# A seven-product SwiGLU in a two-layer decoder: another order for the begun pair, a shorter lead for weights, and three moved sums

## The chip, the cores and the metric

The kernel runs on one core of one Trainium2 chip. A core has a matrix engine (PE; its weight loads are shown apart as PEld), a vector engine (DVE), a scalar engine (ACT), a general engine (POOL) and a queue processor (SP) that mostly starts transfers. Each engine works through its own instructions strictly in the order in which the program lists them; engines meet only at semaphores. The metric is the device time of one execution in microseconds; the smaller, the better. Times of one kernel lie close together (955.57 to 956.49 us in three runs of the kernel before).

## The reference

Two decoder layers over 512 tokens of width 1024. Layer 0 mixes tokens by causal pooling, layer 1 by differential attention; behind each mixer stands a dense SwiGLU block, and each of the four steps ends in a LayerNorm of `ALPHA * x + step(x)`. The change touches the SwiGLU blocks, which both layers have:

```python
D_MODEL = 1024; SEQ = 512; DEPTH = 2; D_FF = 2816
def _swiglu(x, w_gate, w_up, w_down):
    return (jax.nn.silu(x @ w_gate) * (x @ w_up)) @ w_down
...
        x = _layernorm(ALPHA * x + h, ln_mix_g[i], ln_mix_b[i])
        x = _layernorm(ALPHA * x + _swiglu(x, w_gate[i], w_up[i], w_down[i]), ln_ffn_g[i], ln_ffn_b[i])
```

All of it is float32.

## The kernel before

**Float32 in two parts.** PE multiplies in a format with fewer bits, so each float32 operand is held as a high part (a copy that is rounded, made by ACT: a CAST) and a low part (the rest, made by DVE as a subtraction: a "low"). A product then takes three matmuls: high by high, high by low, low by high. So every block of 128x1024 weights costs one transfer from HBM (into a buffer named `raw`, of which there are five), one CAST on ACT, one low on DVE, and it occupies one of six pairs of weight buffers until PE has used it.

**Seven products in place of eight.** The 2816 hidden rows are 22 blocks of 128. Block k and block k + 11 make up pair k (k from 0 to 10). Pairs 0 to 2 are computed plainly (`plain`: a gate and an up product for each block). Pairs 3 to 10 (`SPLIT`) go through `strassen(k)`. There the two halves of the model width, gate against up, and the two halves of the tokens are combined in Strassen's manner: seven half products replace eight. Their weights are sums of rows of the weight array, which DVE forms ("sum" steps, L660, in place in the raw buffers). Their right operands are quarters of x, or sums of quarters, which `sums_of_x` prepares once (parts `xs`, made at L717 and L720). The seven are named P1, Q5, P6, Q3, P7, P2, Q4, and this is also their order in `GATE`. Each half product is 24 matmuls (`half_product`).

**Banks.** A half product accumulates into a bank of PSUM: P1, P6, P7 and Q4 into A, Q5 and Q3 into C, P2 into B. Between two products on one bank the running sum is read out: ACT copies A to B after P1 (L965), A to `hid` after P6 (L969) and C to `hid` after Q5 (L967); DVE takes C after Q3 (L971) and A after P7 (L973). The next product on that bank waits for that reading. Pair 3 is "begun" in the early part of the block, where tokens of the first half are ready before the others: its P1 and P2 are computed there, so the loop in `strassen(3)` has five products left: Q5, P6, Q3, P7, Q4.

**Who makes weights when.** A weight block that is ready to multiply is a "chunk"; chunks are numbered in the order in which PE takes them. In layer 0 and layer 1 alike 0 to 13 are the plain ones and the early two, 14 to 18 the five of pair 3, 19 to 25 those of pair 4, and so on, seven a pair, to 67. `steps` is a list, written by hand for a pair, of sums, CASTs and lows. `ahead(upto)` carries out steps until all chunks below `upto` are done. After product j, `strassen` calls `ahead(j + 6)`. What this emits lands in DVE's and ACT's queues ahead of whatever is emitted later, the reading of later banks included.

**Other work in the same queues.** `sum_terms(k)` (L774, L775) adds blocks of the down weights and ACT stores the results to HBM (L779). `sum_hidden(k)` makes two sums of hidden rows for the down products: four DVE operations on 128x256 (L800 to L803), a CAST on ACT (L805), a low on DVE (L807) and a store by ACT (L809). Its tiles `u` and `v` have one buffer each. It is queued after every pair in `behind`, and `catch_up` carries each queued job one step further after every product. The down products (L1023) come last in the block. ACT starts its own transfers, and its queue stands still while such a start waits.

**The end of the pooling mixer.** `ready(n)` prepares the first n weight rows while the mixer ends. `norm(0, 3)` (L217) normalizes the last quarter of the tokens, after POOL has raised the variance to a power (L208).

## Time and profile before

| | us |
|---|---|
| median of three runs | 956.07 |
| the profiled execution | 954.77 |
| its span (first to last instruction) | 953.0 |
| PE busy in the span | 925.6 (97%) |
| DVE busy | 801.3 (84%) |
| ACT busy | 521.2 (55%) |
| POOL busy | 126.1 (13%) |

The profiled execution is 1.3 us under the median and 1.8 us over its own span. PE is busy nearly throughout, so a time can change by PE's idle time and by the clock at which PE runs (the granted clock, whose mean is 0.988 of full). Layer 0's SwiGLU lies between 35 and 372 us of the span, layer 1's from about 606 us to the end; attention lies between them. A view of waits tells for which engine's instruction another engine stood idle; a timeline gives start, length and the idle time just before; the chain is the work that set the end, in order of time.

### The profile page before, as it was taken

How to read it: one execution, taken by the hardware profiler on the slowest of the kernel's cores; microseconds unless marked ns; L12 is line 12 of the kernel's file. 1: busy time of each engine (PE TensorE's matmuls, PEld its weight loads, DVE VectorE, ACT ScalarE, POOL GpSimd, SP SyncE). 2: the span in 40 equal slices, each digit the busy share in tenths (PEclk: the TensorE clock that was granted, in tenths of full speed). 3: DMA queues.
4: the chain of work that ended last, by engine and by line, in shares of the span. 5: the costliest groups of instructions: out<-in, count | busy, mean ns of one | idle time of the engine just before them, and what ended most of it. 6: DMA issues, size and time to landing. Idle time of an engine off the chain costs nothing.

```text
span 953.0 us, 15072 instructions
## 1 busy us (share of the span) xinstructions
PE 925.6 (97%) x5758; PEld 831.5 (87%) x5758; DVE 801.3 (84%) x1172; ACT 521.2 (55%) x826; POOL 126.1 (13%) x152
## 2 busy tenths in 40 slices
PE   9999969999999999999999999999889999999996
PEld 8898869999998888888888888988789999988885
DVE  8978988999978687968989777879979999878678
ACT  6652444555455456776878854832435455564450
POOL 4111111110000201100111100211111110001101
PEclk9999989999999999999999999999989999999998
DMA  8497898886868988876676521595888985778952
GB/s 235 165 283 244 232 304 250 261 243 189 281 196 258 358 283 249 224 190 169 145 153 161 168 71 67 171 319 168 270 246 262 266 261 205 252 254 271 362 173 88
DMA packets 86614, 213.21 MB, mean 224 GB/s; under 512 B 15204, under 2 KB 26724, under 8 KB 86542
## 3 DMA queue, kind: packets, MB, share of 16 engines
q1 hardware_dynamic: 43996, 119.26, 38.3%
q0 software_dynamic: 18768, 58.20, 25.3%
q10 hardware_dynamic: 23778, 34.78, 9.9%
q8 instruction: 45, 0.74, 0.3%
q14 instruction: 27, 0.22, 0.1%
HBM read 175.50 MB, written 36.72 MB: 223 GB/s over the span
## 4 chain that ended last, share of the span: by engine, by line
PE 82%; DVE 12%; issue 3%; ACT 2%; DMA 0%; POOL 0%; DVEq 0%; ACTq 0%; POOLq 0%
PE A L867 19%; PE P L1023 13%; PE C L867 8%; PE Q L1023 6%; PE B L867 5%; PE va L1173 2%; PE s L1242 2%; PE q L158 2%; PE q L160 2%; PE k L158 2%; PE k L160 2%; PE q L159 2%; PE k L159 2%; DVE raw L660 2%; PE vc L1173 1%
## 5 line engine op out<-in xcount | busy, mean ns | idle before, releaser
L660 DVE TENSOR_TENSOR raw<-raw,raw 128x1024 f32<-128x1024 f32 x64 | 78.1, 1221 | 1.0
L132 ACT CAST xs<-hid 128x512 fp32r<-128x512 f32 (+1 forms) x60 | 34.7, 581 | 24.3 <-DVE hid L837 24.3
L133 DVE TENSOR_TENSOR xs<-hid,xs 128x512 fp32r<-128x512 f32 (+1 forms) x60 | 38.4, 642 | 7.8 <-ACT xs L132 7.8
L1262 ACT ACTIVATE p<-p,mn 128x128 f32<-128x128 f32 (+3 forms) x64 | 35.2, 552 | 14.1 <-DVE mn L1257 14.1
L258 ACT ACTIVATE y<-pt,bT,gT 128x128 f32<-128x128 f32 x72 | 27.0, 455 | 27.9 <-PE pt L244 27.8
L768 POOL DMA_DIRECT2D b<-in_wall x20 | 14.0, 706 | 183.7 <-DMA tsum<-b 122.5
L829 POOL DMA_DIRECT2D xs<-ssum x24 | 17.4, 725 | 142.3 <-PE Q L1023 68.8
L208 POOL TENSOR_TENSOR rs<-rs,mhalf 128x1 f32<-128x1 f32 x16 | 12.1, 760 | 141.5 <-DVE rs L207 102.0
L768 POOL DMA_DIRECT2D hid<-in_wall x24 | 18.7, 824 | 88.1 <-DMA tsum<-hid 45.4
L1257 DVE CUSTOM_DVE_ANT_0 p<-s,bias 128x128 f32<-128x128 f32 (+3 forms) x64 | 28.0, 485 | 1.1 <-PE s L1242 1.1
L971 DVE TENSOR_TENSOR hid<-C,hid 128x512 f32<-128x512 f32 x16 | 11.0, 690 | 17.7 <-PE C L867 15.1
L133 DVE TENSOR_TENSOR xt<-y,xt 128x512 fp32r<-128x512 f32 x18 | 12.2, 689 | 13.7 <-ACT xt L132 13.7
L867 PE MATMUL A<-xt,g_18h 128*128 128x256 f32 x32 | 9.3, 392 | 14.7 <-DVE hid L973 14.7
L978 ACT ACTIVATE sg<-A 128x512 f32<-128x512 f32 x16 | 9.6, 597 | 24.9 <-PE A L867 24.9
L199 DVE BATCH_NORM_STATS2 st<-res 128x6 f32<-128x512 f32 x32 | 22.2, 694 | 1.1
L805 ACT CAST v<-u 128x512 fp32r<-128x512 f32 x22 | 13.7, 621 | 14.7 <-DVE u L803 14.7
L717 ACT CAST xs<-hid 128x1024 fp32r<-128x1024 f32 x8 | 8.4, 1051 | 23.7 <-DVE hid L729 17.3
L867 PEld LDWEIGHTS A<-xt,g_18h 128*128 128x128 f32 x32 | 7.7, 294 | 15.1 <-DVE hid L973 15.1
L967 ACT COPY hid<-C 128x512 f32<-128x512 f32 x16 | 9.4, 586 | 20.5 <-PE C L867 20.5
L769 POOL DMA_DIRECT2D hid<-in_wall x12 | 14.8, 1233 | 41.8 <-DMA hid<-in_wall 41.8
L701 DVE TENSOR_TENSOR hid<-sg,u 128x512 f32<-128x512 f32 x12 | 8.2, 684 | 12.5 <-PE u L160 7.3
L1276 DVE SCALAR_TENSOR_TENSOR p<-p,sm,p 128x128 f32<-128x128 f32 (+3 forms) x32 | 17.6, 551 | 1.1
(1218 smaller groups left out, 3653.3 us busy)
## 6 DMA issues: line engine op xcount, KB each, us to landing
raw<-in_wall SPq DMA_DIRECT2D x126, 512.0 KB, 4.9
r<-tsum SPq DMA_DIRECT2D x40, 512.0 KB, 4.5
hid<-in_wall POOLq DMA_DIRECT2D x36, 512.0 KB, 5.9
b<-in_wall POOLq DMA_DIRECT2D x30, 512.0 KB, 6.0
r<-in_wall SPq DMA_DIRECT2D x30, 512.0 KB, 5.5
tsum<-hid ACTq DMA_DIRECT2D x24, 512.0 KB, 6.6
ssum<-v ACTq DMA_DIRECT2D x22, 512.0 KB, 3.7
tsum<-b ACTq DMA_DIRECT2D x20, 512.0 KB, 5.4
```

The costliest lines, as they stand in the source:

```text
L132: nc.scalar.copy(dst_h, src)
L133: (low or nc.vector).tensor_tensor(dst_l, src, dst_h.bitcast(F32), op=ALU.subtract)
L158: nc.tensor.matmul(acc, ah, bh, start=start, stop=False)
L159: nc.tensor.matmul(acc, ah, bl, start=False, stop=False)
L160: nc.tensor.matmul(acc, al, bh, start=False, stop=stop)
L660: tt(t, raws[pair[0]], raws[pair[1]], op=ALU.add)
L768: nc.gpsimd.dma_start(out=t[:, j], in_=src[:, j])
L867: nc.tensor.matmul(o, w[:, c], x[:, kk, :], start=start and f + kk + e == 0, stop=stop and (f, kk, e) == (1, 3, 2), skip_group_check=True,)
L1023: nc.tensor.matmul(accs[s], x[:, k, r], y[:, c], start=first and k == 0 and e == 0, stop=last and k == m - 1 and e == 2, skip_group_check= ...
L1173: nc.tensor.matmul(accs[s], a[:, kk, t], b[:, c], start=p in ("P1", "Q5", "P2") and kk + e == 0, stop=p in ("Q4", "Q3", "P2") and (kk, e) ...
L1257: nc.vector.tensor_tensor_reduce(out=p, in0=accs[c], in1=biases[h][:, w - 1 :: -1] if w < S else biases[h][:, ::-1], op0=ALU.add, op1=ALU. ...
L1262: nc.scalar.activation(p, p, AF.Exp, bias=mn[:, q, c : c + 1], scale=-1.0, accum_out=sm[:, q, c : c + 1],)
```

## The change

It has six parts; all but the fourth and fifth act in both layers.

1. The five products left of pair 3 now come in the order of `BEGUN`: P6, Q5, P7, Q3, Q4. With the banks as they are, A, C, A, C, A: before it was C, A, C, A, A. The silu of the finished gate part moves to the head of `strassen(3)`. The steps of this pair are listed in a new order that fits.
2. The lead of the weights shrinks: `ahead(j + 4)` after all products of pair 3 and after P1, Q5 and P6 of the others; `j + 5` after Q3, P7, P2 and Q4 up to pair 9; `j + 6` there in pair 10.
3. `sum_hidden(2)` and `sum_hidden(3)` are no longer queued behind their own pairs, but behind Q3 of pair 6 and of pair 8 (`SPARED`).
4. In layer 0 `ready(7)` before `norm(0, 3)` prepares the weights of pair 3's P1 there, as `w6`, and no longer as chunk 4 behind it.
5. P1 of the begun pair takes its 24 matmuls in another order (`high_first`): all 16 with the high weights, then the 8 with the low ones. (In layer 1 too.)
6. In `sums_of_x` the low of P6's operand comes one step earlier and that of P7's one later.

```diff
@@ -49,6 +49,8 @@
 SPLIT = (3, 4, 5, 6, 7, 8, 9, 10)
 EARLY = (2, 1)
 GATE = ("P1", "Q5", "P6", "Q3", "P7", "P2", "Q4")
+SPARED = {2: 6, 3: 8}
+BEGUN = ("P6", "Q5", "P7", "Q3", "Q4")
 PAIRS = [(0, 2), (2, 2), (4, 2), (6, 2), (8, 2), (10, 1)]
 
 
@@ -520,6 +522,7 @@
         ready(6)
         summed(3, 0, 1)
         spread_of(0, 3)
+        ready(7)
         norm(0, 3)
 
         nc.scalar.copy(far, lines_bank[:HEADS, NEAR - 1 :])
@@ -625,18 +628,22 @@
                 c = [row(4 * k + i) for i in range(4)]
                 todo = [(c[0], ()), (c[0], (c[0], c[1])), (c[0], (c[0], c[2])), (c[2], ())]
                 todo += [(c[1], (c[1], c[2])), (c[3], ()), (c[0], (c[0], c[3]))]
-                for m, chunk in enumerate(todo):
-                    if (k, m, "pair") not in number:
-                        number[k, m, "pair"] = len(chunks)
-                        chunks.append(chunk)
-                if k > SPLIT[0]:
+                begun = k == SPLIT[0]
+                for p in BEGUN if begun else GATE:
+                    m = GATE.index(p)
+                    number[k, m, "pair"] = len(chunks)
+                    chunks.append(todo[m])
+                if not begun:
                     step("cast", number[k, 0, "pair"])
-                for w in (
+                order_of = (
+                    "sum 1, cast 1, sum 4, cast 3, cast 4, low 1, sum 2, cast 2, low 2, low 4, "
+                    "low 3, sum 6, cast 6, low 6"
+                    if begun else
                     "low 0, sum 1, cast 1, sum 4, cast 3, cast 4, low 1, sum 2, cast 2, low 3, "
                     "low 2, sum 6, cast 5, cast 6, low 4, low 5, low 6"
-                ).split(", "):
-                    if k > SPLIT[0] or w[-1] not in "05":
-                        steps.append((w[:-2], number[k, int(w[-1]), "pair"]))
+                )
+                for w in order_of.split(", "):
+                    steps.append((w[:-2], number[k, int(w[-1]), "pair"]))
             uses = {}
             for kind, j in steps:
                 c, pair = chunks[j]
@@ -737,9 +744,9 @@
                 yield
                 tt(r3, r3, r2, op=ALU.add)
                 high(3, r3)
+                low(1, r2)
+                yield
                 low(2, r0)
-                yield
-                low(1, r2)
                 yield
                 low(3, r3)
                 yield
@@ -856,20 +863,23 @@
             def both(t):
                 return t.rearrange("p (f t) -> p f t", f=2)
 
-            def half_product(acc, j, left, start, stop):
+            def half_product(acc, j, left, start, stop, high_first=False):
                 h, l = halves[j]
                 xh, xl = left
-                for f in range(2):
-                    o = acc[:, f * 256 : (f + 1) * 256]
-                    for kk in range(4):
-                        c = slice((4 * f + kk) * P, (4 * f + kk + 1) * P)
-                        for e, (w, x) in enumerate(((h, xh), (h, xl), (l, xh))):
-                            nc.tensor.matmul(
-                                o, w[:, c], x[:, kk, :],
-                                start=start and f + kk + e == 0,
-                                stop=stop and (f, kk, e) == (1, 3, 2),
-                                skip_group_check=True,
-                            )
+                terms_of = ((h, xh), (h, xl), (l, xh))
+                places = [(f, kk) for f in range(2) for kk in range(4)]
+                if high_first:
+                    todo = [(f, kk, w, x) for w, x in terms_of for f, kk in places]
+                else:
+                    todo = [(f, kk, w, x) for f, kk in places for w, x in terms_of]
+                for i, (f, kk, w, x) in enumerate(todo):
+                    c = slice((4 * f + kk) * P, (4 * f + kk + 1) * P)
+                    nc.tensor.matmul(
+                        acc[:, f * 256 : (f + 1) * 256], w[:, c], x[:, kk, :],
+                        start=start and i == 0,
+                        stop=stop and i == len(todo) - 1,
+                        skip_group_check=True,
+                    )
 
             lefts = {
                 "P1": [quarter(0, i, 0) for i in range(2)],
@@ -909,7 +919,7 @@
                             behind.append(sum_hidden(0))
                 if not lo:
                     bankA, bankB = bank(f"A{layer}_{SPLIT[0]}"), bank(f"B{layer}")
-                    half_product(bankA, number[SPLIT[0], 0, "pair"], lefts["P1"], True, False)
+                    half_product(bankA, number[SPLIT[0], 0, "pair"], lefts["P1"], True, False, True)
                     if "P1" in late:
                         late["P1"]()
                     nc.scalar.copy(both(g3), both(bankA))
@@ -935,7 +945,7 @@
                     weight_sums()
                 if f == 3:
                     load_terms(3)
-                if f % 2:
+                if f % 2 and k not in SPARED:
                     behind.append(sum_hidden(k))
 
             def strassen(k):
@@ -949,14 +959,12 @@
                 def tile_of(i):
                     return keep.tile([P, S], F32, tag="y", name=f"sg{layer}_{k}_{i}", bufs=2)
 
-                for m, p in enumerate(GATE):
-                    if begun and p in ("P1", "P2"):
-                        if p == "P2":
-                            g0 = g3
-                            nc.scalar.activation(g0, g0, AF.Silu)
-                        continue
+                if begun:
+                    g0 = g3
+                    nc.scalar.activation(g0, g0, AF.Silu)
+                for p in BEGUN if begun else GATE:
                     acc = banks[names[p]]
-                    j = number[k, m, "pair"]
+                    j = number[k, GATE.index(p), "pair"]
                     half_product(
                         acc, j, lefts[p], p in ("P1", "Q5"), p in ("Q4", "Q3", "P2")
                     )
@@ -976,8 +984,10 @@
                     else:
                         g1 = tile_of(1)
                         nc.scalar.activation(both(g1), acc, AF.Silu)
-                    ahead(j + 6)
+                    ahead(j + (4 if begun or p in ("P1", "Q5", "P6") else 5 if k < SPLIT[-1] else 6))
                     catch_up()
+                    if p == "Q3" and k in SPARED.values():
+                        behind.extend(sum_hidden(i) for i in SPARED if SPARED[i] == k)
                     if p == "P2":
                         nc.scalar.activation(both(g0), acc, AF.Silu)
                     elif p == "Q4":
@@ -985,7 +995,8 @@
                         tt(second, both(g1), second, op=ALU.mult)
                 if k < HALF - 1:
                     weight_sums()
-                behind.append(sum_hidden(k))
+                if k not in SPARED:
+                    behind.append(sum_hidden(k))
 
             f = early
             while f < FB:
```

Three places show what this does to the queues. The first is DVE's queue around the reading of bank A after P7 of pair 3, in layer 0 (in layer 1 the rows are alike). `g0_19l` is a low of chunk 19; a row that writes `raw` and reads two `raw` is a sum. Before:

```order
L801 TENSOR_TENSOR hid0_531<-hid0_531 128x256
L802 TENSOR_TENSOR u0_2_1252<-hid0_531 128x256
L803 TENSOR_TENSOR u0_2_1252<-u0_2_1252,hid0_531 128x256
L660 TENSOR_TENSOR raw20_1078<-raw20_1078,raw21_1135 128x1024
L660 TENSOR_TENSOR raw21_1135<-raw21_1135,raw22_1198 128x1024
L666 TENSOR_TENSOR g0_20l_1285<-raw20_1078,g0_20h_1284 128x1024
L971 TENSOR_TENSOR hid0_531<-C0_3_1211,hid0_531 128x2x256
L660 TENSOR_TENSOR raw20_1078<-raw20_1078,raw22_1198 128x1024
L666 TENSOR_TENSOR g0_22l_1289<-raw22_1198,g0_22h_1288 128x1024
L666 TENSOR_TENSOR g0_21l_1323<-raw20_1078,g0_21h_1322 128x1024
L807 TENSOR_TENSOR v0_2_1253<-u0_2_1252,v0_2_1253 128x2x256
L973 TENSOR_TENSOR hid0_531<-hid0_531,A0_3_678 128x2x256
```

And after the change, where L981 is the line that was L973, and L979 the line that was L971:

```order
L667 TENSOR_TENSOR raw16_924<-raw16_924,raw19_1033 128x1024
L673 TENSOR_TENSOR g0_18l_1269<-raw16_924,g0_18h_1268 128x1024
L981 TENSOR_TENSOR hid0_537<-hid0_537,A0_3_678 128x2x256
L673 TENSOR_TENSOR g0_19l_1272<-raw20_1078,g0_19h_1271 128x1024
L979 TENSOR_TENSOR hid0_537<-C0_3_1205,hid0_537 128x2x256
L667 TENSOR_TENSOR raw20_1078<-raw20_1078,raw21_1195 128x1024
L667 TENSOR_TENSOR raw21_1195<-raw21_1195,raw22_1263 128x1024
L673 TENSOR_TENSOR g0_20l_1330<-raw20_1078,g0_20h_1329 128x1024
L667 TENSOR_TENSOR raw20_1078<-raw20_1078,raw22_1263 128x1024
L673 TENSOR_TENSOR g0_22l_1334<-raw22_1263,g0_22h_1333 128x1024
L673 TENSOR_TENSOR g0_21l_1368<-raw20_1078,g0_21h_1367 128x1024
L994 TENSOR_TENSOR hid0_537<-g3_0_551,hid0_537 128x2x256
```

The reading of A moved up past the lows of chunks 19 to 22, three sums, the reading of C and all of `sum_hidden(2)`.

The second place is ACT's queue from the end of pair 6 into pair 7, in layer 0. Before:

```order
L982 ACTIVATE sg0_6_0_2067<-B0_679 128x512
L978 ACTIVATE sg0_6_1_2093<-A0_6_1870 128x512
L663 CAST g0_45h_2096<-raw35_1936 128x1024
L663 CAST g0_46h_2099<-raw32_1731 128x1024
L965 COPY B0_679<-A0_7_2107 128x512
L779 DMA tsum0_533<-b0_7_1664 128x2x512 x2
L967 COPY hid0_531<-C0_7_2108 128x2x256
L663 CAST g0_47h_2176<-raw36_1968 128x1024
L805 CAST v0_6_2144<-u0_6_2143 128x2x256
L969 COPY hid0_531<-A0_7_2107 128x2x256
```

And after:

```order
L812 CAST v0_2_2018<-u0_2_2017 128x2x256
L992 ACTIVATE sg0_6_0_2047<-B0_679 128x512
L986 ACTIVATE sg0_6_1_2082<-A0_6_1844 128x512
L973 COPY B0_679<-A0_7_2089 128x512
L816 DMA ssum0_540<-v0_2_2018 512x1x256
L786 DMA tsum0_539<-b0_7_1635 128x2x512 x2
L975 COPY hid0_537<-C0_7_2090 128x2x256
L670 CAST g0_45h_2155<-raw35_1970 128x1024
L670 CAST g0_46h_2158<-raw32_1739 128x1024
L812 CAST v0_6_2124<-u0_6_2123 128x2x256
L977 COPY hid0_537<-A0_7_2089 128x2x256
```

The CASTs of chunks 45 and 46 went from before the three readings of banks to between the second and the third, and the CAST and the store of the spared `sum_hidden(2)` came in; chunk 47's CAST follows behind.

The third place is DVE's queue at the end of the pooling mixer. Before:

```order
L205 BN_AGGR mv0_3_515<-st0_3_511 128x2
L207 TENSOR_SCALAR rs0_3_517<-mv0_3_515 128x1
L217 TENSOR_SCALAR res_67<-res_67,mv0_3_515,rs0_3_517 128x1024
L666 TENSOR_TENSOR g0_4l_573<-raw6_330,g0_4h_572 128x1024
L666 TENSOR_TENSOR g0_5l_576<-raw7_482,g0_5h_575 128x1024
```

And after:

```order
L207 BN_AGGR mv0_3_515<-st0_3_511 128x2
L209 TENSOR_SCALAR rs0_3_517<-mv0_3_515 128x1
L135 TENSOR_TENSOR w6l_523<-raw6_330,w6h_522 128x1024
L219 TENSOR_SCALAR res_67<-res_67,mv0_3_515,rs0_3_517 128x1024
L673 TENSOR_TENSOR g0_5l_579<-raw7_482,g0_5h_578 128x1024
```

The low of P1's weights changed places with the normalization of the last quarter.

## The prediction

> **What bounds the kernel now.** I read the page first, then the waits of PE, then stretches of the clock and the chain of waits, and last the timelines of DVE and ACT.

> ```profile
> span 953.0 us, 15072 instructions
> PE 925.6 (97%) x5758; PEld 831.5 (87%) x5758; DVE 801.3 (84%) x1172; ACT 521.2 (55%) x826; POOL 126.1 (13%) x152
> PE 82%; DVE 12%; issue 3%; ACT 2%; DMA 0%; POOL 0%; DVEq 0%; ACTq 0%; POOLq 0%
> ```

> PE is busy for all but 27.4 us of its span, so the change, which takes no matmul away, can win idle time and clock only. Two waits hold most of the idle time (columns: total, times, longest):

> ```profile
> PE A L867 <- DVE hid L973: 14.7, 2, 7.3
> PE A L867 <- DVE g_4l L666: 2.3, 1, 2.3
> PEld o L158 <- DVE mn L1257: 2.5, 7, 0.4
> ```

> The first is Q4 of the begun pair, once in each layer, waiting until DVE has read bank A after P7. The second is P1 of that pair in layer 0, waiting for its low weights. Such idle time also costs clock. Stretches (length, PE, PEld, DVE, ACT, POOL, then the granted clock), and pieces of the chain:

> ```profile
> 46.45:49.86 3.41, 3.29 (x15) 3.29 (x16) 2.40 (x4) 0.00 (x0) 0.41 (x1) 0.50 0.95 292
> 124.95:131.78 6.83, 3.23 (x15) 3.23 (x16) 6.38 (x7) 1.68 (x2) 1.47 (x2) 0.50 0.63 182
> 691.57:698.39 6.82, 4.46 (x21) 4.46 (x22) 5.17 (x6) 0.63 (x1) 1.16 (x3) 0.50 0.85 246
> 372.00:606.00 234.00, 233.73 (x1246) 194.12 (x1245) 188.99 (x404) 169.71 (x351) 30.26 (x35) 1.00 0.59 148
> ```

> ```profile
> 46.57 4.34 PE A L867 x22
> 51.78 2.87 PE B L867 x24
> 54.65 2.88 PE g L683 x24
> 128.55 7.43 PE A L867 x48
> 150.38 5.76 PE A L867 x48
> 693.93 7.97 PE A L867 x48
> ```

> After each of the three gaps the clock stands at 0.50 for a while. 24 matmuls take 2.88 us at full clock. So the 22 after the first gap lost 4.34 - 22/24 x 2.87 = 1.7, and the 48 after the two others 7.43 - 5.76 = 1.7 and 7.97 - 5.76 = 2.2.

> **What the begun order removes.** The five products start with this row and follow without a gap, so three of them end at 109.55 + 3 x 2.88 = 118.2 and four at 121.1.

> ```profile
> 109.55 0.40 PE L867 MATMUL C<-xs,g_14h 128*128 128x256 f32 x2
> 115.69 1.22 DVE L666 TENSOR_TENSOR g_18l<-raw,g_18h 128x1024 fp32r<-128x1024 f32 x1
> 117.96 0.42 DVE L800 TENSOR_TENSOR u<-hid 128x256 f32<-128x256 f32 x1
> 119.55 2.48 DVE L660 TENSOR_TENSOR raw<-raw,raw 128x1024 f32<-128x1024 f32 x2
> 121.95 1.22 DVE L666 TENSOR_TENSOR g_20l<-raw,g_20h 128x1024 fp32r<-128x1024 f32 x1
> 127.21 0.68 DVE L807 TENSOR_TENSOR v<-u,v 128x512 fp32r<-128x512 f32 x1
> 127.81 0.68 DVE L973 TENSOR_TENSOR hid<-hid,A 128x512 f32<-128x512 f32 x1
> 95.00 1.05 ACT L663 CAST g_14h<-raw 128x1024 fp32r<-128x1024 f32 x1 [5.62 <-DVE raw L660]
> ```

> Before, P7 is the fourth (121.1), DVE reads it at 127.81, and Q4 can go at 128.5: 7.4 late. DVE is not waiting there; its queue is full. After, P7 is the third, and DVE has only to be through with the low of chunk 18. What stands ahead of that low is, by the order, the same set of operations as before, which ended at 115.69, but three of them now wait for ACT. The low of chunk 14 follows its own sum and so waits for a CAST of 1.05 (1.2 us with the hand-overs, some 0.2 more for its weight buffer); the low of chunk 18 likewise (1.1); the third wait was there before. The low thus starts at 115.69 + 2.5 = 118.2, and DVE reads A at 118.2 + 1.2 = 119.4, done at 120.1. Q4 is due at 121.1. So the whole stall goes, with 1.0 us to spare, in both layers: 14.7 us, and with it the slow clock, 1.7 + 2.2.

> From there on the walk goes through pair 4, since DVE is late: low 19, C, two sums, low 20, sum, lows 22 and 21 lead from 120.1 to about 129.0; P6 of pair 4 needs low 21 at 121.1 + 3 x 2.88 = 129.7. Next come the two gate products of `hid` and `sum_terms`, to 131.7. ACT's store of those sums waits for this and the copy of bank C stands behind it, done at 132.8; Q3 is due at 132.6. I take 0.2 us of new wait a layer.

> **What the lead costs later.** One regular pair, with T the end of Q4 of the pair before (173.4 here):

> ```profile
> 173.46 0.60 ACT L978 ACTIVATE sg<-A 128x512 f32<-128x512 f32 x1 [0.98 <-PE A L867]
> 175.55 0.68 DVE L984 TENSOR_TENSOR hid<-sg,hid 128x512 f32<-128x512 f32 x1
> 179.22 0.59 ACT L967 COPY hid<-C 128x512 f32<-128x512 f32 x1 [1.47 <-PE C L867]
> 182.09 0.59 ACT L969 COPY hid<-A 128x512 f32<-128x512 f32 x1 [0.55 <-PE A L867]
> 185.04 0.69 DVE L971 TENSOR_TENSOR hid<-C,hid 128x512 f32<-128x512 f32 x1 [1.28 <-PE C L867]
> ```

> DVE's only idle time in these 20.16 us is the 1.28. The operations are the same after the change, so a regular pair keeps it. With the new order I get: L994 at T + 2.1 as now; the sums of terms done at T + 4.7, so the copy of C done at T + 5.7 (Q3: T + 8.6); sums of hidden rows to T + 6.3, a sum to T + 7.4, the CAST of that sum and of `v` to T + 9.0, the copy of A at T + 9.6 (P7 is due at T + 11.5, 1.9 to spare). DVE reads C at T + 11.6, then two lows, and A at T + 14.5, done 2.1 before Q4. No wait.

> In pairs 7 and 9 DVE arrives 2.2 us later, since a spared sum (1.6 + 0.6, by 117.96 to 119.55 and 127.21 to 127.81) now stands before the end of pairs 6 and 8: the copy of A is done at T + 11.75, and P7 waits 0.25. That CAST of `v` also waits until the spared store, which leaves at T + 4.9, has landed, as `v` has one buffer. Landings (least, median, most) of `v`, the first row in the regular pairs, the second around the begun pair, and of rows of weights in the regular pairs:

> ```profile
> DMA to landing us min/median/max: 3.2/3.3/3.9
> ```

> ```profile
> DMA to landing us min/median/max: 3.4/5.5/7.6
> ```

> ```profile
> DMA to landing us min/median/max: 3.5/4.9/5.4
> ```

> The pairs in question are regular: landed at T + 8.2, ahead of the CAST at T + 10.5. I cost it at nothing; the cover goes if landing takes over 5.6, and at 7.6 P7 waits 2 us more, four times. DVE catches up by its 1.28 within the next pair. In pair 10 two lows of down weights and two of `hid` (about 3.5 us) now stand between the readings of C and A, which is then done at T + 17.6; Q4 is due at T + 17.3: 0.3.

> New waits: 0.2 + 0.25 + 0.25 + 0.3 = 1.0 a layer, 2.0 in all. Each is a difference of two sums of many terms, so between 0 (all covered) and about 1 apiece (8 in all). At 0.4 us, as in attention, waits leave the clock at 1.00.

> [...]

> **The low of P1 in layer 0.**

> ```profile
> 43.69 0.15 DVE L207 TENSOR_SCALAR rs<-mv 128x1 f32<-128x1 f32 x1
> 44.57 0.81 DVE L217 TENSOR_SCALAR res<-res,mv,rs 128x1024 f32<-128x1024 f32 x1 [0.73 <-POOL rs L208]
> 45.30 1.22 DVE L666 TENSOR_TENSOR g_4l<-raw,g_4h 128x1024 fp32r<-128x1024 f32 x1
> ...
> 61.98 1.22 DVE L236 TENSOR_TENSOR res<-res,gb 128x1024 f32<-128x1024 f32 x1
> ```

> ```profile
> 39.26 0.42 SPq L187 DMA_DIRECT2D gb<-in_lnb  x1
> ```

> The low now runs from 43.8 to 45.0, partly in DVE's 0.73 of waiting for POOL; the normalization slips by 0.5 to 45.1 to 45.9. P1 was due at 46.57 - 2.3 - 2 x 0.12 = 44.0 and asks for lows after 16 matmuls, at 45.9: no wait, end at 46.9, where the transposes need the normalized rows (45.9). The order of the 24 costs nothing: 24 matmuls by parts take 2.88 too (54.65). So PE gains 2.3 + 1.7 = 4.0. It stays ahead if DVE and ACT follow, and they do: their next work is the transposed tiles. Between nothing kept and all, I take all. The gamma and beta loads start one row of weights later than at 39.3, and are first needed at 62.0. The swap in `sums_of_x` moves a low by 1.14 us, and both stand before their products: nothing.

> **The sum.** 14.7 + 1.7 + 2.2 + 4.0 - 2.0 = 20.6 us. From the profiled execution, 954.77, this makes 934.2; from the median, which is 1.3 above it, 956.07 - 20.6 = 935.5.

> **The rivals.**
> 1. The front gain does not carry: DVE is nearly without gaps from there to the begun pair, and DMA engines are 0.95 busy at 46 to 50 us. Then 4.0 less: 939.5. Against it: DVE's gaps before the begun pair end with PE's results, or with a silu of them:

> ```profile
> 77.18 0.69 DVE L701 TENSOR_TENSOR hid<-sg,u 128x512 f32<-128x512 f32 x1 [0.95 <-PE u L160]
> 89.41 0.69 DVE L701 TENSOR_TENSOR hid<-sg,u 128x512 f32<-128x512 f32 x1 [1.61 <-ACT sg L700]
> ```

> 2. Short waits cost clock or the store of `v` lands late in pairs 7 and 9. Eight waits at 1.7 of clock are 13.6 (949.1); four landings at 7.6 are 8 (943.5), or with the clock 15 (950). For it: 2.3 us were enough for the clock. Against it: the clock of 1.00 in attention. [...]
> 3. The change doesn't do what it says: DVE reaches bank A too late all the same. With 1.0 to spare, a DVE 3 us later in both layers leaves two gaps of 2 with 1.7 of clock each: 7.4 less, 943. With as much delay as now, only the 4.0 is left: 952.
> 4. Slower: the third row of weights of each pair is asked for later. Its buffer comes free with a low that moves to T + 8.7 (now about T + 2), and the sum that needs it is due at T + 16.3: a lead of 7.6 us. Landing takes 3.5 to 5.4, so I see no wait. DVE's 1.28 covers the first excess; beyond 8.9 us every pair loses the rest. To eat 20.6 us over 14 pairs, 1.5 each, landings must take 10.4 throughout; at 10.6 the time is 935.5 + 14 x 1.7 = 959.

> **How the numbers follow.** No change can be told from one within 0.2% (1.9 us). My forecast has 0.62 (933 to 938), rival 1 0.12 (938 to 941), rival 2 0.11 (943 to 950), rival 3 0.08 (943 to 952), rival 4 and other slower ends 0.05 (959), no change 0.02. The low end, 932.5, is the gain without any new wait, 956.07 - 22.6 = 933.5, less 1 for the spread of the runs. The high end, 944, takes in rivals 1 and the nearer ends of 2 and 3, and leaves out under 0.2. Faster: 0.62 + 0.12 + 0.11 + 0.08 = 0.93.

> **What would show it.** Right: PE's wait for the reading of A after P7 is gone, the clock has no stretch at 0.50 between 46 us and the tail, P1's matmuls end about 4 us earlier, and DVE keeps an idle time near 1.3 before the reading of C. Wrong: PE's waits for ACT's copies of A or C sum to over 3 us, a CAST of `v` waits for a DMA, or DVE waits for a DMA at a sum of rows.

## The result, and the profile after

The kernel after takes 939.68 us (median of six runs, 938.56 to 942.77), beside 956.28 for the kernel before on the same chip (six runs, 954.72 to 956.79). The ratio is 0.9834, with a 95% interval of 0.9818 to 0.985: faster by 1.7%, or 16.6 us. The forecast was 935.5, a gain of 20.6; the measured time lies within the range, and 4.0 us of the gain are missing. The profiled execution took 938.56 us, the shortest of the six. Its span and busy times, from the page:

```profile
span 936.8 us, 15062 instructions
PE 923.9 (99%) x5758; PEld 828.1 (88%) x5758; DVE 801.2 (86%) x1172; ACT 517.6 (55%) x826; POOL 127.1 (14%) x152
```

PE's idle time has gone from 27.4 to 12.9 us. DVE and ACT do nearly as much work as before. PE's waits in the SwiGLU blocks (total, times, longest):

```profile
PE A L877 <- DVE hid L981: 0.9, 2, 0.6
PE A L877 <- ACT hid L977: 0.8, 5, 0.2
PE C L877 <- ACT hid L975: 0.6, 1, 0.6
PE g L690 <- ACT xt L134: 0.2, 1, 0.2
```

The 14.7 us at the reading of A after P7 and the 2.3 at P1 are gone; L981 still stands here, but for pair 10, where a new wait was forecast. And the clock (length, PE, PEld, DVE, ACT, POOL, granted clock, DMA share, GB/s):

```profile
7.51:932.52 925.01, 918.35 (x5736) 822.86 (x5735) 795.45 (x1165) 512.86 (x819) 124.84 (x140) 1.00 0.74 228
```

No stretch at 0.50 is left between the start and the tail. So all that was to go has gone. Where the 16.2 us between the two spans come from, and where some are lost again, is seen in the starts of PE's products (the first row of each product in the two timelines of PE; the lead is the time before minus the time after):

| start of | before | after | lead of after |
|---|---|---|---|
| the first stretch at full clock | 5.49 | 7.51 | (starts later) |
| the second group of pooling matmuls with low weights | 7.24 | 8.06 | -0.82 |
| the transposes behind P1, layer 0 | 50.74 | 47.58 | 3.16 |
| u of block 0, second half of the tokens | 57.36 | 54.69 | 2.67 |
| second product of the begun pair | 112.42 | 109.75 | 2.67 |
| Q4 of the begun pair | 128.55 | 118.95 | 9.60 |
| P1 of pair 4 | 132.94 | 121.90 | 11.04 |
| first down product, layer 0 | 274.06 | 265.24 | 8.82 |
| first product of the begun pair, layer 1 | 674.93 | 665.98 | 8.95 |
| Q4 of it | 693.93 | 677.49 | 16.44 |
| P1 of pair 4 | 698.85 | 680.37 | 18.48 |
| first down product, layer 1 | 839.97 | 823.79 | 16.18 |

The execution after came to the full clock 2.0 us later and was 0.8 behind with the pooling matmuls. Layer 1 is as forecast up to P1 of pair 4: 7.5 for the stall and 2.0 for the clock. Then 2.3 us are lost up to the down products, where 1.0 was forecast. Layer 0 loses 2.2 at the same place, and it also gains less at the stall: 6.9, since three products of its begun pair start late (by 0.19, 0.11 and 0.26), and 1.4 for the clock, of which it had lost less before.

### The profile page after: what moved, and what is told of

The parts are those of the page before. It is cut to its first block, busy times and chain, and to the rows that moved or that the text cites. A ratio compares the mean times of both kernels' runs of the same rounds, so it can differ in the third digit from the quotient of the medians.

```text
span 936.8 us, 15062 instructions
## 1 busy us (share of the span) xinstructions
PE 923.9 (99%) x5758; PEld 828.1 (88%) x5758; DVE 801.2 (86%) x1172; ACT 517.6 (55%) x826; POOL 127.1 (14%) x152
## 5 line engine op out<-in xcount | busy, mean ns | idle before, releaser
L775 POOL DMA_DIRECT2D b<-in_wall x20 | 14.0, 705 | 179.6 <-DMA tsum<-b 83.3
L210 POOL TENSOR_TENSOR rs<-rs,mhalf 128x1 f32<-128x1 f32 x16 | 12.9, 806 | 142.1 <-DVE rs L209 97.5
L812 ACT CAST v<-u 128x512 fp32r<-128x512 f32 x22 | 13.6, 616 | 10.7 <-DVE u L810 10.7
L776 POOL DMA_DIRECT2D b<-in_wall x10 | 12.3, 1230 | 51.4 <-DMA b<-in_wall 44.5
L979 DVE TENSOR_TENSOR hid<-C,hid 128x512 f32<-128x512 f32 x16 | 11.0, 689 | 8.6 <-PE C L877 8.6
L708 DVE TENSOR_TENSOR hid<-sg,u 128x512 f32<-128x512 f32 x12 | 8.2, 686 | 11.6 <-PE u L162 6.3
L135 POOL TENSOR_TENSOR sql<-sq,sqh 128x512 fp32r<-128x512 f32 x7 | 9.3, 1323 | 60.5 <-ACT sqh L134 60.5
L814 DVE TENSOR_TENSOR v<-u,v 128x512 fp32r<-128x512 f32 x22 | 15.1, 686 | 1.4 <-ACT v L812 0.7
```

The costliest lines, as they stand in the source:

```text
L135: (low or nc.vector).tensor_tensor(dst_l, src, dst_h.bitcast(F32), op=ALU.subtract)
L775: nc.gpsimd.dma_start(out=t[:, j], in_=src[:, j])
L776: nc.gpsimd.dma_start(out=t[:, 0], in_=src[:, :, 1], accum_op=ALU.add)
```

## The experiments

### The order of the begun pair, undone

```diff
-BEGUN = ("P6", "Q5", "P7", "Q3", "Q4")
+BEGUN = ("Q5", "P6", "Q3", "P7", "Q4")
...
-"sum 1, cast 1, sum 4, cast 3, cast 4, low 1, sum 2, cast 2, low 2, low 4, low 3, sum 6, cast 6, low 6"
+"sum 1, cast 1, sum 4, cast 3, cast 4, low 1, sum 2, cast 2, low 3, low 2, sum 6, cast 6, low 4, low 6"
...
-                low(1, r2)
-                yield
-                low(2, r0)
+                low(2, r0)
+                yield
+                low(1, r2)
```

> The five products of the begun pair in the old order again (Q5, P6, Q3, P7, Q4), with the old list of steps and the old order of two lows of the sums of x; shorter lead, sparing and front are kept. Theory: what kept DVE from bank A was the lead, so that the reading of A comes behind low 18, the reading of C and low 19 only, and is waiting when P7 ends. Q4 then waits for one reading alone, the 0.68 us of its row and some 0.3 of hand-over, 1 us in each layer in place of 7.3, too short for the clock: 939.7 + 2 = 941.7 us (941 to 943). Rival: the alternation of banks is what removed the stall, and without it both gaps of 7.3 and their slow clock (1.7 + 2.2) come back: 957 to 958.

Measured: 941.43 us (ratio to the kernel before 0.9845, 0.9821 to 0.987). The waits at Q4 of the begun pair, from the timeline of PE in layer 0 and in layer 1:

```profile
121.99 0.50 PE L877 MATMUL A<-xt,g_18h 128*128 128x256 f32 x2 [0.78 <-DVE hid L981]
681.90 0.50 PE L877 MATMUL A<-xt,g_18h 128*128 128x256 f32 x2 [0.78 <-DVE hid L981]
```

With the banks A, A again, each wait is 0.78 and not 7.3, and the clock stays at 1.00 up to the tail. The rival falls: the alternation of the banks is not what removed the stall.

### The lead, undone

```diff
-                    ahead(j + (4 if begun or p in ("P1", "Q5", "P6") else 5 if k < SPLIT[-1] else 6))
+                    ahead(j + 6)
```

> The new order of the begun pair is kept, the lead is six products everywhere as before. Theory (the lead counts): low 19, two sums and low 20, 4 x 1.2 us, stand ahead of DVE's reading of A again. In layer 1 that reading started at 675.72 with 1.1 us to spare, in layer 0 at 118.12 with 0.1: waits of 3.7 and 4.7 before Q4, each with about 2 us of slow clock, so 8.4 + 4 = 12 us: 952 (949 to 954). Rival (the order alone is enough): no stretch at 0.50, and 939 to 941.

Measured: 947.47 us (0.9912, 0.988 to 0.9944). The profiled execution is the longest of the four (950.05; the shortest is 944.29). Layer 0 and layer 1, timeline of PE:

```profile
120.93 0.51 PE L877 MATMUL C<-xs,g_17h 128*128 128x256 f32 x2 [2.46 <-ACT hid L975]
126.15 0.50 PE L877 MATMUL A<-xt,g_18h 128*128 128x256 f32 x2 [0.58 <-DVE hid L981]
683.21 0.50 PE L877 MATMUL C<-xs,g_17h 128*128 128x256 f32 x2 [1.26 <-ACT hid L975]
688.43 0.79 PE L877 MATMUL A<-xt,g_18h 128*128 128x256 f32 x2 [2.08 <-DVE hid L981]
```

A stall is back with the new order in place, so the lead decides. Its size was put too high: part of it is taken one product earlier, at Q3, which waits for ACT's copy of C, behind the CASTs of chunks 18 and 19, which the longer lead puts ahead of it; and each layer has one short stretch at 0.50 (3.41 us) where I had reckoned with two.

### The front, undone

```diff
-        ready(7)
         norm(0, 3)
...
-half_product(bankA, number[SPLIT[0], 0, "pair"], lefts["P1"], True, False, True)
+half_product(bankA, number[SPLIT[0], 0, "pair"], lefts["P1"], True, False)
```

> Parts 4 and 5 undone: in layer 0 the low of P1 stands behind the normalization again, and P1 takes its 24 matmuls in the mixed order. Theory: of the 4.0 us that PE wins at the front, 2.4 reach the end of layer 0, since DVE and ACT do not follow it by as much: 0.5 goes at the second half of the first gate product, 0.6 within the begun pair's products, 0.5 at Q3 of pair 4. So undoing costs 2.4: 942.1 us; the begun pair's products in layer 0 then start 2.88 us apart, and Q3 of pair 4 waits as little as in layer 1 (0.1). Rival A: all of it is kept to the end: 943.7. Rival B: nothing is kept: 939.7.

Measured: 940.41 us (0.9843, 0.9824 to 0.9861), not told apart from the kernel after. The theory's 942.1 is missed; the nearest is rival B. In the trace P1 waits its 2.3 us and the clock has its stretch at 0.50, so the 4.0 are really lost there; something in the kernel after must take most of them back later. The two traces show a part of that: the begun pair of layer 0 starts at 106.87 in the kernel after and at 109.44 here, so the kernel after leads by 2.6 us; P1 of pair 4 starts at 121.90 and 123.83 (1.9), the down products at 265.24 and 266.90 (1.7). The traced execution of the kernel after is its shortest, and by the medians no lead is left.

### The sparing, undone

```diff
-SPARED = {2: 6, 3: 8}
+SPARED = {}
```

> Part 3 undone: the sums of hidden rows 2 and 3 are queued behind their own pairs again. Theory: DVE has four operations of 0.42 us and a low of 0.69 more before pair 4, twice, about 2.2 us each; with 0.1 (layer 0) and 1.1 us (layer 1) to spare before Q4 of the begun pair, that makes waits of 1.5 and 0.5 there and up to 2.2 more around P6 and Q3 of pair 4, less the 0.3 each that pairs 7 and 9 no longer wait: 2 to 2.5 us a layer, 944.3 (943 to 946; with slow clock behind the longer ones up to 950). Rival: DVE's idle time makes up for it, and only the waits of pairs 7 and 9 go: 938.4.

Measured: 943.8 us (0.9873, 0.9857 to 0.9888), as the theory had it. Q4 of the begun pair waits 1.60 in layer 0 and 0.49 in layer 1, and P6, Q3 and P7 of pair 4 wait 0.27, 0.71 and 0.60 in layer 1. The clock stays at 1.00.

### The lead alone

The kernel after with the order, the sparing and the front undone as above.

> The kernel before with the shorter lead alone: old order of the begun pair, nothing spared, old front, old order of the two lows of the sums of x (only the silu at the head of the begun pair stays moved). Theory (what undoing one part costs adds up): the kernel after, 939.7, plus 1.7 for the order, 4.1 for the sparing and 0.7 to 2.4 for the front make 946.2 to 947.9 us; so the lead alone is worth 8 to 10 of the 16.6. Rival (the parts lean on each other): without the sparing and the new order, the reading of bank A is late again by enough for the slow clock behind both begun pairs, 950 to 953.

Measured: 943.53 us (0.9865, 0.985 to 0.9881), better than the theory's sum. So the lead alone (with the moved silu) brings some 12.5 of the 16.6 us. Q4 of the begun pair, layer 0 and layer 1:

```profile
124.27 0.50 PE L876 MATMUL A<-xt,g_18h 128*128 128x256 f32 x2 [2.96 <-DVE hid L980]
684.34 0.51 PE L876 MATMUL A<-xt,g_18h 128*128 128x256 f32 x2 [1.30 <-DVE hid L980]
```

What undoing one part costs doesn't add up. A difference between the traces: with the new front and no sparing, DVE waited 4.6 us for a DMA in layer 0, and with the old front it doesn't. The next two runs show what that is.

### The same kernel again, and one without the new waits

> The kernel after, unchanged, on the same chip as the others of this set and with another trace. Theory: 939.7 us (939 to 940.5); the spread between its executions comes from the start, so that from the first product of the begun pair in layer 0 to the end the two traces agree within 0.3 us, while the time at which PE comes to it differs by up to 1 us. Rival: the spread lies in the waits of the pairs, and the two traces part there by 1 us or more.

Measured: 940.96 us (five runs, 937.67 to 944.45; 0.9853, 0.9836 to 0.987). The two traces part at the start (1.0 us), but also by 0.5 at P7 of the begun pair in layer 0 and 0.7 at pair 10 in layer 1, so neither guess has the whole of it.

The other kernel moves three things:

```diff
-                if k < HALF - 1:
+                if k < HALF - 1 and not begun:
                     weight_sums()
-                if k not in SPARED:
+                if k not in SPARED and k not in SPARED.values():
                     behind.append(sum_hidden(k))
...
                     catch_up()
+                    if p == "P1" and k - 1 in SPARED.values():
+                        behind.append(sum_hidden(k - 1))
+                    if p == "Q5" and k - 1 == SPLIT[0]:
+                        weight_sums()
...
-ahead(j + (4 if begun or p in ("P1", "Q5", "P6") else 5 if k < SPLIT[-1] else 6))
+ahead(j + (4 if begun or p in ("P1", "Q5", "P6") else 5 if k < SPLIT[-1] or p == "Q3" else 6))
```

> The kernel after with the causes of its new waits moved: the sums of hidden rows 6 and 8 are queued one product later (behind P1 of the next pair), the block of down weights summed at the end of pair 3 is summed behind Q5 of pair 4, and in pair 10 DVE does one down weight and one row of x less ahead of the reading of A. Theory: each of the seven waits named (0.58, 0.16, 0.16, 0.30 us in layer 0, 0.16, 0.16, 0.58 in layer 1) costs its length and 0.25 besides, as the starts of PE's products say, 3.8 us in all, of which 3 to 3.8 come back: 936 to 937 us. Rival A: a wait costs its listed length only, 2.1 us come back: 937.6. Rival B: the waits turn up elsewhere, since DVE has the same work: 939 to 940.

Measured: 936.74 us (0.98, 0.9786 to 0.9813): faster than the kernel after, as the theory says, though a new loss stands in its trace. Why a wait of 0.16 cost more than 0.16 is seen in the kernel after at P7 of pair 7 (timeline of PE):

```profile
194.61 0.28 PE L877 MATMUL C<-xs,g_43l 128*128 128x256 f32 x1
195.05 0.51 PE L877 MATMUL A<-xs,g_44h 128*128 128x256 f32 x2 [0.16 <-ACT hid L977]
195.40 0.28 PE L877 MATMUL A<-xs,g_44l 128*128 128x256 f32 x1
195.51 0.40 PE L877 MATMUL A<-xs,g_44h 128*128 128x256 f32 x2
```

Matmuls overlap in this trace: the two at 194.13 and 194.25 start 0.12 apart, and each is listed as busy for 0.28. The product was due at 194.73, so it is 0.32 late, though only 0.16 of that is listed as idle; and the first rows then take 0.11 longer (0.35 to the next low in place of 0.24). Together that is 0.42.

The new loss in that kernel's trace is in layer 0 and comes from a DMA. The first line is DVE's sum for the second block of down weights, which waits for the load of that block. The next is PE's wait in P6 of the begun pair for a low of the sums of x, and the last two are the stretch of the clock with that wait and the one after it:

```profile
73.49 0.69 DVE L781 TENSOR_TENSOR hid<-hid 128x512 f32<-128x512 f32 x1 [5.27 <-DMA hid<-in_wall]
```

```profile
PE A L877 <- DVE xs L727: 2.0, 1, 2.0
```

```profile
105.79:109.20 3.41, 1.42 (x9) 0.99 (x8) 2.94 (x4) 1.53 (x3) 1.34 (x2) 1.00 0.63 210
109.20:112.62 3.42, 3.42 (x19) 3.42 (x18) 2.86 (x3) 0.53 (x2) 1.17 (x2) 0.50 0.78 283
```

The same sum stands in the kernel before without a wait, in the kernel after and in its repetition with waits of 2.1 and 2.7:

```profile
70.96 0.69 DVE L774 TENSOR_TENSOR hid<-hid 128x512 f32<-128x512 f32 x1
```

```profile
70.67 0.69 DVE L781 TENSOR_TENSOR hid<-hid 128x512 f32<-128x512 f32 x1 [2.12 <-DMA hid<-in_wall]
```

DVE reaches this sum 2.4 us earlier than before (68.55 instead of 70.96), but the load it needs is later, so DVE gets away only 0.3 us earlier than before. Here is where much of the front's gain goes: PE keeps its lead, while the lows and sums that it will need in the begun pair come no earlier. What waits 5.3 us here also waited 4.1 to 5.2 in the kernels with the order, the lead and the sparing undone, which had the new front; not in those with the old front. In those three traces PE then waited 0.7, 1.9 and 1.3 us for a low of the sums of x, which it doesn't in the kernel after. So what undoing the order, the lead and the sparing cost holds some of this wait, and that is a reason why the costs don't add up to what the lead alone, which has the old front, leaves.

### Longer waits

```diff
+COPIES = {(0, 5): 10, (0, 6): 9, (0, 8): 10, (1, 5): 10, (1, 6): 8, (1, 8): 10}
...
                     elif p == "P6":
-                        nc.scalar.copy(first, acc)
+                        for _ in range(COPIES.get((layer, k), 1)):
+                            nc.scalar.copy(first, acc)
```

> ACT repeats its copy of bank A after P6 in three pairs of each layer (10, 9 and 10 copies in pairs 5, 6 and 8 of layer 0; 10, 8 and 10 in layer 1), so that P7 waits for the last one: a copy every 0.48 us, the first now 1.9 us early, makes waits of 2.4 (four), 1.9 and 1.5 us. Theory: a wait costs its length and 0.25, 14.5 us in all; and the clock is granted in stretches of 3.413 us that lie on a grid set at the start, a stretch with 2.08 us or more of PE's idle time is followed by one at 0.50, a stretch with 1.60 or less is not. So a wait of 2.4 costs clock only if enough of it lies in one stretch: some of the four do, some don't, each at about 1.5 us of loss: 955 to 960 us. Rival: the length of a wait alone decides, and all four waits of 2.4 are followed by a stretch at 0.50, the shorter ones by none.

Measured: 974.64 us (one run). The waits came out longer than planned: 21.0 us over six, up to 4.1. All six, and a wait of 1.8 for the copy of C in pair 10, were followed by stretches at 0.50, so length and share of a stretch were not told apart. The two bounds on idle time lie closer together for it, though. Stretches of 3.41 us on the grid of the clock, each with the one that follows it. In this kernel:

```profile
178.02:181.44 3.42, 1.54 (x13) 1.34 (x12) 0.31 (x1) 3.23 (x7) 1.23 (x1) 1.00 0.76 230
181.44:184.85 3.41, 2.32 (x11) 2.32 (x12) 2.34 (x3) 1.95 (x3) 0.00 (x0) 0.50 0.95 261
843.62:847.04 3.42, 1.59 (x14) 1.39 (x13) 3.23 (x7) 1.47 (x2) 0.00 (x0) 1.00 0.69 261
847.04:850.45 3.41, 3.41 (x19) 3.41 (x18) 3.41 (x4) 2.62 (x5) 0.00 (x0) 0.50 0.28 59
```

And in the kernel without sparing:

```profile
119.25:122.66 3.41, 1.81 (x16) 1.64 (x15) 2.30 (x4) 2.04 (x3) 0.00 (x0) 1.00 1.06 396
122.66:126.07 3.41, 3.41 (x28) 3.41 (x29) 3.38 (x5) 0.64 (x2) 0.00 (x0) 1.00 0.85 337
```

In the kernel with longer waits, with PE idle for 1.83 us of a stretch (3.42 - 1.59), the next one was at half clock; in the kernel without sparing, with 1.60 (3.41 - 1.81), it kept the full one.

### The store held back

The late load is POOL's last one of the second block. Its answers by line, in the kernel before and in the kernel after:

```profile
L769 POOL DMA_DIRECT2D hid<-in_wall x1: 1227/1227/1227, 59.0 to 59.0; - x1
DMA to landing us min/median/max: 5.7/5.7/5.7
```

```profile
L776 POOL DMA_DIRECT2D hid<-in_wall x1: 1227/1227/1227, 60.3 to 60.3; - x1
DMA to landing us min/median/max: 10.2/10.2/10.2
```

It is issued 1.4 us later and takes 4.5 longer. Beside it ACT starts the store of the first block's sums at 60.65 and 63.32, which it did at 63.33 and 65.81 before. The first start, in the timeline of ACT before and after:

```profile
63.33 0.40 ACTq L779 DMA_DIRECT2D tsum<-hid  x1
60.65 0.40 ACTq L786 DMA_DIRECT2D tsum<-hid  x1
```

So a DVE that is ahead has brought the store forward onto the load. The next three kernels test this.

```diff
             def sum_terms(k):
...
                 yield
+                if (layer, k) == (0, 0):
+                    yield
                 dst = tsum[:, k // 2, :, term_slice(k)].rearrange("(j r) p t -> p j r t", j=2)
```

> The kernel after, with one thing moved: in layer 0 ACT starts the store of the first block of summed down weights one step of its queue later, about 65 us instead of 60.7 and 63.3. Theory: that store now falls together with POOL's last load of the second block (issued at 60.3, landed 10.2 us later, against 5.7 in the kernel before), and DVE, which the front has made earlier, waits 2.1 to 5.3 us for it, a different time in each execution; this is where the front's gain and the spread of the executions go. With the store held back the load lands in 6 to 7 us, DVE waits under 1 us, the products of the begun pair in layer 0 start 2.88 us apart and Q3 of pair 4 waits about 0.1 there: 937.7 to 939 us where the kernel after has 939.7 and 941.0 in two sets. Rival: it is the weight rows of SP's queue that slow the load; landing and wait stay as they are, 939.7 to 941.

Measured: 937.76 us (five runs, 936.44 to 939.15; 0.9816, 0.98 to 0.9832). The load, and DVE at the sum:

```profile
L776 POOL DMA_DIRECT2D hid<-in_wall x1: 1227/1227/1227, 60.4 to 60.4; - x1
DMA to landing us min/median/max: 6.1/6.1/6.1
```

```profile
67.91 0.69 DVE L781 TENSOR_TENSOR hid<-hid 128x512 f32<-128x512 f32 x1
```

The load lands after 6.1 us, DVE doesn't wait, and PE has no listed wait left around the begun pair of layer 0 nor at Q3 of pair 4 (which starts 0.11 us late, and 0.74 in the kernel after). The store went out only about 2 us later (62.9), which was enough; SP issued its two rows of weights at 57.3 and 58.4, ahead of the load as in the kernel after (57.9 and 59.0), so the rival falls. Over all fourteen traces: with the new front and the early store (0.3 us after the load's issue to 1.7 ahead of it; seven traces) the load took 9.4 to 12.1 us, with the store held back (2.4 to 3.2 after; three traces) 6.1 to 7.2, and with the old front (4.1 to 4.8 after; three traces) 5.7 to 7.3. The fourteenth is an exception; it comes below. In time the step is 1.9 us against one set of the kernel after and 3.2 against the other, and the interval of its ratio overlaps with that of the first set.

> The kernel with its waits moved (936.7) and the store held back as well. In its trace DVE waited 5.3 us for that load, P6 of the begun pair in layer 0 then waited 2.0 for a low of the sums of x, and a stretch at 0.50 followed: about 3.4 us. Theory: these go, 933.5 to 935 us. Rival: the load lands late for another reason, and 936.7 stays.

Measured: 933.97 us (932.76 to 935.76; 0.9779, 0.9763 to 0.9796), the fastest of all and as the theory said. Page, clock and all of PE's waits:

```profile
span 931.7 us, 15072 instructions
PE 921.0 (99%) x5758; PEld 827.6 (89%) x5758; DVE 800.9 (86%) x1172; ACT 518.5 (56%) x826; POOL 127.1 (14%) x152
```

```profile
8.00:918.00 910.00, 909.49 (x5709) 817.60 (x5708) 785.45 (x1147) 513.35 (x819) 122.99 (x138) 1.00 0.75 230
```

```profile
PE warm L366 <- POOL ident masks.py:199: 1.9, 1, 1.9
PE g L690 <- ACT xt L134: 0.2, 1, 0.2
PE pt L246 <- DVE res L219: 0.2, 1, 0.2
```

PE is idle for 0.51 of 910 us. The step from 937.76 to 933.97 is the new waits without the collision: 3.8 us, what lengths and 0.25 apiece had given.

> The kernel with its waits moved (936.7) and parts 4 and 5 undone. Theory: with the old front DVE comes to the second block of down weights after it has landed, so that wait (5.3 in the trace) and what follows in layer 0 (3.4 us) go, and the 2.3 of P1's wait with 1.7 of clock come back: 937.3 us (936.5 to 938.5), so as things stand the front is worth nothing. Rival: the front's 4.0 are kept to the end, and undoing it makes 940.7.

Measured: 936.49 us (935.05 to 936.88; 0.9801, 0.9787 to 0.9816), against 936.74 with the new front: beside the early store the front is worth nothing, as the third experiment said. In this trace the load took 9.9 us although the store was issued 3.1 after it; two of SP's rows were issued in its first 1.3 us. So the store is not all that can slow it. DVE, later with the old front, didn't wait. Against the fastest kernel, which has the new front and the store held back, it is 936.49 - 933.97 = 2.5 us (the old front with the store held back was not run).

In this trace (935.05 us, the shortest of the four) the old front costs less than 4.0 for another reason: P1 waits its 2.29 us, but no stretch at 0.50 follows. PE's row, and two stretches on the grid of the clock:

```profile
47.00 0.39 PE L876 MATMUL A<-xt,g_4l 128*128 128x256 f32 x1 [2.29 <-DVE g_4l L672]
43.14:46.55 3.41, 1.57 (x14) 1.37 (x12) 2.61 (x5) 2.25 (x6) 1.88 (x3) 1.00 0.72 285
46.55:49.97 3.42, 2.97 (x25) 2.97 (x26) 2.73 (x4) 0.00 (x0) 0.56 (x2) 1.00 0.90 304
```

The wait is split by the grid, 1.84 us idle in one stretch and 0.45 in the next. With longer waits, a shorter one of 1.83 that lay within one stretch was followed by half clock. So the length of a wait alone did not decide here, and the wait of 2.3 at P1, which cost its clock in the kernel before (3.41 - 1.24 = 2.17 us idle in one stretch there, in the line below), did not cost it in this execution.

```profile
43.04:46.45 3.41, 1.24 (x11) 1.04 (x9) 2.61 (x6) 1.91 (x5) 2.15 (x3) 1.00 0.70 275
```

> The kernel with its waits moved and the store held back (934.0), with the five products of the begun pair in the old order once more (old list of steps, old order of the two lows). Theory: with the lead short and DVE in time, the old order leaves one wait in each layer, Q4 for the reading of bank A, listed at 0.78 us as in the kernel with the old order and costing its length and 0.25 besides: 2.1 us, 936.1 (935.3 to 937). Rival: DVE makes the order needless, 934.0.

Measured: 935.44 us (934.84 to 935.66; 0.9792, 0.9778 to 0.9805). Q4 of the begun pair waits 0.78 in each layer, as expected, and by the starts of its products PE loses 1.0 us at each of the two places. The intervals of the two ratios overlap a little; the order is worth 1.5 us by the medians.

## Why the prediction was right, and where it was not

**Right.** The prediction had these right: the bound (idle time and clock of PE), the full removal of the stall, the clock that comes back with it, and the walk of DVE to bank A: I had the reading at 1.0 us ahead of need, and in layer 1 it starts at 675.72, is done at 676.4 and is needed at 677.49. In layer 0, where DVE had waited for the late load, it starts only at 118.12 and is done at 118.8, while Q4 was due at 118.7; with the store held back it starts at 116.05, and Q4 is due at 117.83. DVE's two readings in the kernel after:

```profile
118.12 0.68 DVE L981 TENSOR_TENSOR hid<-hid,A 128x512 f32<-128x512 f32 x1
675.72 0.68 DVE L981 TENSOR_TENSOR hid<-hid,A 128x512 f32<-128x512 f32 x1
```

The places of the new waits are also those named (pair 4, 7, 9 and 10), and one more, at P7 of pair 10 in layer 1. Waits this short (0.58 at most) left the clock alone, so rival 2 did not come. What the prediction had cited against that rival could not show it: the waits of 0.4 in attention are waits of the weight loads (PEld), while PE itself was idle for only 0.27 of those 234 us. It was also right that the lead of 7.6 us for the third row of weights was enough (rival 4). DVE keeps 1.29 us of idle time before the reading of C in a regular pair.

**New waits: 2.0 forecast, 4.5 measured.** This term was mis-sized (2.2 in layer 0, 2.3 in layer 1, from the starts of PE's products), and the runs without the waits give 2.9 to 4.2 us back (939.68 and 940.96 against 936.74, 937.76 against 933.97). I compared the end of a copy with the due time of a product and took the difference as the cost. A late start costs 0.1 more in the first rows, and the copies and readings were later than worked out by about 0.1 (pairs 7 and 9) to 0.5 (pair 4 in layer 0, pair 10 in layer 1). Of the lateness in pair 4 of layer 0, 0.63 belongs to the next point: Q3 starts 0.74 late there, and 0.11 with the store held back.

**The front: 4.0 forecast, won, and not carried.** P1 and the transposes behind it came 3.98 us earlier, after allowing for the 0.82 by which this execution started later. The step that failed is "It stays ahead if DVE and ACT follow, and they do: their next work is the transposed tiles". I took this from gaps that end with PE, and did not ask which transfers a faster DVE starts and which it needs. The store of the first sums came onto the load of the second, the load took 4.5 us longer, and DVE lost nearly all that it had won. ACT took a smaller part: the second half of the first gate product behind P1 waits for its CAST of the transposed tiles (0.24 listed), and the lead falls from 3.16 to 2.67. Rival 1 named the outcome, and "DVE waits for a DMA at a sum" is in the list of what would show the forecast wrong, but with the wrong sum in mind (rows of weights for SwiGLU, not the down weights). In the medians the front brings nothing that can be measured (0.7 and -0.5 us against the two sets of the kernel after), and some 2.5 with the store held back.

**Where the missing gain is in the traces.** At the end of layer 1's products the lead is 16.2 us where 20.6 were forecast, so 4.4 are missing. Of these 0.8 are the later start of this execution and 0.5 ACT's CAST behind P1. The late load takes 1.2 (0.56 in the begun pair of layer 0 and 0.63 at Q3 of pair 4; both are gone with the store held back). The other new waits are 4.5 - 0.6 - 2.0 = 1.9 over the forecast. DVE's wait for the load was 1.7 to 5.3 us in the seven traces with the new front and the early store, so the late load is also the likely cause of the wide spread between executions; that the slowest executions (942.77, 944.45) are such is not shown, since they have no trace.

**What the gain was put down to.** The prediction credited the stall to the begun order. Undoing the order alone costs 1.8 or 0.5 us against the two sets of the kernel after, and 1.5 in the fastest kernel; undoing the lead alone costs 7.8 or 6.5, and the lead alone brings 12.5. My own walk had the reason in it, "DVE has only to be through with the low of chunk 18": that is what the shorter lead leaves ahead of the reading. The sum was right and the name on it was wrong.

## What to carry to other kernels

If a reading of a bank comes late in an engine's queue, first count what stands ahead of it: a shorter lead can do more than a new order of products. When an engine gets faster, list the transfers that its work starts and the transfers that it needs, and see which now run together; a gain at the front can end at a DMA that nobody waited for. When sizing a short wait of PE, compare starts of products rather than the listed idle time.
